# Seven block products in place of eight for part of a down projection, with one weight sum by an accumulating DMA

## The chip, the cores and the metric

The kernel runs on one core of a Trainium2 chip. The metric is the device time of one execution in microseconds; shown is the median of three runs. All values are 32-bit floats. The work is one layer of a streaming encoder for 256 tokens (two token tiles of 128) of width 2048.

## The reference

The layer is a set of token mixers with an output projection, then a feed-forward half with width 5632. The change touches the last product of the feed-forward half and what leads to it and from it:

```python
def rms_norm(x, g):
    return x * lax.rsqrt(jnp.mean(x * x, axis=-1, keepdims=True) + EPS) * g
...
h = h + rms_norm(mixed @ w_out, g_post_mix)
u = rms_norm(h, g_pre_ffn)
f = silu(u @ w_gate) * (u @ w_up)              # [256, 5632]
h = h + rms_norm(f @ w_down, g_post_ffn)       # w_down [5632, 2048]
```

## The kernel before

A product of 32-bit precision is made of three products of float32r parts: each operand is cut into a high part (a cast) and a low part (the operand less the high part), and the matmuls are high with high, high with low, low with high (`product`, lines 206 to 211).

All weights pass as one stream of chunks. A chunk is 256 rows by 512 columns, held as `[128, 2, 512]`, 512 KB. `load` (line 154) puts it into one of four buffers `raw` by a DMA on SP's queue; `prep` (line 158) makes its parts, in the down projection with one cast on ScalarE (line 168, tile `hi`) and one subtraction on VectorE (line 169, tile `lo`), into one of `NPARTS = 5` pairs. Each chunk feeds 12 matmuls: two token tiles, two rows of 128, three part products. When a chunk's matmuls are issued, `release` tops up the stream: the next chunk is prepared as long as it is less than five chunks ahead of the last released one, and loads run up to four chunks ahead of preparation. ScalarE, VectorE and TensorE take their instructions in the order in which the program issues them; the order on SP's and POOL's queues is set by a scheduler when the program is built.

Other work (evacuations, transposes, norms) is cut into steps by generators, which the class `Side` issues between chunks. In the feed-forward half, `up_job` (from line 1097) multiplies gate and up, transposes the result on TensorE into two PSUM banks and cuts it into the parts `fh[i]`, `fl[i]`, for each of the 11 row blocks `i` of 512 rows. `xt` holds the residual `h` in SBUF from the middle of the kernel to the end.

The down projection goes over four column blocks `b` of 512. For each, 22 chunks are multiplied into a pair of accumulators, one per token tile. `y_job` then squares the sums on ScalarE (line 1138) and multiplies them by the gain on VectorE (line 1141). In the last column block the last four chunks are taken for token tile 0 first and then for tile 1, so that the norm and the last step (`final`, line 1154) of tile 0 run beside the matmuls of tile 1.

## Time and profile before

| what | us |
|---|---|
| median of three runs | 1085.11 (1084.42 to 1085.63) |
| span of the profiled execution | 1084.9 |
| TensorE busy (matmuls) | 1071.0 |
| VectorE busy | 685.4 |
| ScalarE busy | 606.4 |
| 16 DMA engines, share of the span of the load queue | 57.2% |

The profile is of one execution. No time of its own is listed for it beside its span; the span lies among the three times, 0.2 us under their median. In the lines, PE is TensorE, PEld its weight load, DVE VectorE, ACT ScalarE, POOL GpSimd, and SP the engine that issues the loads (SPq is its queue). L168 is line 168 of the kernel. The page is read from the busy shares to the chain that ended last, and a stretch by its windows, its waits ("A waited for B: us in total, times, longest") and its timeline (start, duration, engine, line, operation, and the idle time ahead of it with what ended it).

### The profile page before, as it was taken

How to read it: one execution, taken by the hardware profiler on the slowest of the kernel's cores; microseconds unless marked ns; L12 is line 12 of the kernel's file. 1: busy time of each engine (PE TensorE's matmuls, PEld its weight loads, DVE VectorE, ACT ScalarE, POOL GpSimd, SP SyncE). 2: the span in 40 equal slices, each digit the busy share in tenths (PEclk: the TensorE clock that was granted, in tenths of full speed). 3: DMA queues.
4: the chain of work that ended last, by engine and by line, in shares of the span. 5: the costliest groups of instructions: out<-in, count | busy, mean ns of one | idle time of the engine just before them, and what ended most of it. 6: DMA issues, size and time to landing. Idle time of an engine off the chain costs nothing.

```text
span 1084.9 us, 13175 instructions
## 1 busy us (share of the span) xinstructions
PE 1071.0 (99%) x4826; PEld 887.6 (82%) x4826; DVE 685.4 (63%) x988; ACT 606.4 (56%) x867; POOL 8.8 (1%) x19
## 2 busy tenths in 40 slices
PE   8999999999999999999999999999999999999996
PEld 6888888888888888888888888888888888888885
DVE  6576998976687765665556656565565444444544
ACT  6768757678854855545455454555554434343432
POOL 0000001010000000000000000000000000000000
PEclk9999999999999999999999999999999999999998
DMA  8854554546572465555555555555556555565552
GB/s 313 293 188 157 186 175 155 194 166 214 194 236 94 155 227 183 192 194 184 185 194 192 192 183 190 194 189 193 183 192 218 194 195 193 194 193 194 194 192 78
DMA packets 58097, 207.03 MB, mean 191 GB/s; under 512 B 6448, under 2 KB 6832, under 8 KB 57776
## 3 DMA queue, kind: packets, MB, share of 16 engines
q1 hardware_dynamic: 58032, 206.18, 57.2%
q8 instruction: 38, 0.62, 0.2%
q14 instruction: 27, 0.22, 0.1%
HBM read 204.06 MB, written 2.10 MB: 190 GB/s over the span
## 4 chain that ended last, share of the span: by engine, by line
PE 98%; DMA 1%; DVE 0%; ACT 0%; SPq 0%; issue 0%; ACTq 0%
PE acc L209 32%; PE acc L210 32%; PE acc L211 32%; PE bank L1106 1%; PE bank L352 1%; DMA w<-xT 1%; PE bank L975 0%; PE bank L662 0%; PE bank L713 0%; DVE xt L1154 0%; PE bank L714 0%; PE bank L663 0%; PE bank L515 0%; PE bank L516 0%; PE bank L433 0%; PE bank L691 0%
## 5 line engine op out<-in xcount | busy, mean ns | idle before, releaser
L209 PE MATMUL acc<-hi,w 128*128 128x512 f32 x1360 | 533.4, 392 | 3.3 <-ACT hi L770 1.8
L210 PE MATMUL acc<-lo,w 128*128 128x512 f32 x1360 | 530.5, 390 | 0.3 <-DVE lo L771 0.3
L211 PE MATMUL acc<-hi,w 128*128 128x512 f32 x1360 | 530.6, 390 | 0.0
L169 DVE TENSOR_TENSOR lo<-raw,hi 128x1024 fp32r<-128x1024 f32 x198 | 241.6, 1223 | 186.9 <-ACT hi L168 186.3
L165 DVE SCALAR_TENSOR_TENSOR lo<-raw,par,hi 128x512 fp32r<-128x512 f32 x344 | 242.7, 748 | 184.7 <-ACT hi L164 184.7
L164 ACT ACTIVATE hi<-raw,par 128x512 fp32r<-128x512 f32 x344 | 229.5, 717 | 208.0 <-PE acc L211 208.0
L168 ACT CAST hi<-raw 128x1024 fp32r<-128x1024 f32 x198 | 207.0, 1050 | 211.5 <-PE acc L211 192.9
L209 PEld LDWEIGHTS acc<-hi,w 128*128 128x128 f32 x1360 | 256.0, 188 | 56.5 <-ACT hi L770 4.3
L211 PEld LDWEIGHTS acc<-hi,w 128*128 128x128 f32 x1360 | 255.8, 188 | 53.8 <-DVE w L982 0.5
L210 PEld LDWEIGHTS acc<-lo,w 128*128 128x128 f32 x1360 | 256.0, 188 | 53.3 <-DVE lo L771 1.2
L594 DVE SCALAR_TENSOR_TENSOR w<-u,par,w 128x256 f32<-128x256 f32 x120 | 51.1, 482 | 0.0
L209 PE MATMUL acc<-hi,mh 128*128 128x512 f32 x128 | 50.4, 394 | 0.0
L211 PE MATMUL acc<-hi,ml 128*128 128x512 f32 x128 | 49.9, 390 | 0.0
L210 PE MATMUL acc<-lo,mh 128*128 128x512 f32 x128 | 49.8, 389 | 0.0
L211 PEld LDWEIGHTS acc<-hi,ml 128*128 128x128 f32 x128 | 24.0, 188 | 5.1
L210 PEld LDWEIGHTS acc<-lo,mh 128*128 128x128 f32 x128 | 24.1, 188 | 4.8
L209 PEld LDWEIGHTS acc<-hi,mh 128*128 128x128 f32 x128 | 24.0, 188 | 4.8
L1095 DVE SCALAR_TENSOR_TENSOR s<-acc,rffn,s 128x512 f32<-128x512 f32 x22 | 15.4, 742 | 0.0
L1100 DVE SCALAR_TENSOR_TENSOR s<-acc,rffn,s 128x512 f32<-128x512 f32 x22 | 15.4, 742 | 0.0
L347 ACT ACTIVATE w<-acc,rpre 128x512 f32<-128x512 f32 x22 | 13.8, 684 | 2.2 <-DVE rpre L307 2.2
L1113 DVE TENSOR_TENSOR w<-bank,w 128x512 fp32r<-128x512 f32 x22 | 14.1, 682 | 0.0
L1092 ACT ACTIVATE s<-acc,rffn 128x512 f32<-128x512 f32 x22 | 13.7, 675 | 0.0
(204 smaller groups left out, 425.4 us busy)
## 6 DMA issues: line engine op xcount, KB each, us to landing
raw<-w_up SPq DMA_DIRECT2D x88, 512.0 KB, 3.3
raw<-w_down SPq DMA_DIRECT2D x88, 512.0 KB, 3.3
raw<-w_gate SPq DMA_DIRECT2D x84, 512.0 KB, 3.3
raw<-w_in SPq DMA_DIRECT2D x78, 512.0 KB, 3.4
raw<-w_out SPq DMA_DIRECT2D x32, 512.0 KB, 3.4
xt<-x_tok SPq DMA_DIRECT2D x2, 1024.0 KB, 7.9
w<-w_gate SPq DMA_DIRECT2D x4, 512.0 KB, 5.5
out<-xt SPq DMA_DIRECT2D x8, 256.0 KB, 2.1
```

What stands on the lines that cost most here:

```text
L164: A.activation(hi[:, kk, :], raw[:, kk, :], AF.Copy, scale=g)
L165: V.scalar_tensor_tensor(out=lo[:, kk, :], in0=raw[:, kk, :], scalar=g, in1=hi[:, kk, :].bitcast(F32), op0=ALU.mult, op1=ALU.subtract)
L168: A.copy(out=hi, in_=raw)
L169: V.tensor_tensor(out=lo, in0=raw, in1=hi.bitcast(F32), op=ALU.subtract)
L209: T.matmul(acc, xh(k)[:, ts], hi[:, kk, :], start=first, stop=False)
L210: T.matmul(acc, xh(k)[:, ts], lo[:, kk, :], start=False, stop=False)
L211: T.matmul(acc, xl(k)[:, ts], hi[:, kk, :], start=False, stop=last)
L347: A.activation(dst[:, t, :], acc[t], func, scale=rpre[:, t:t + 1])
L594: V.scalar_tensor_tensor(out=cy[:, n, :], in0=u[:, n, j:j + S], scalar=pv("dw_conv_w", j * 4 + n), in1=cy[:, n, :], op0=ALU.mult, op1=ALU.add)
L1095: V.scalar_tensor_tensor(out=ss[t], in0=acc[t], scalar=rffn[:, t:t + 1], in1=ss[t], op0=ALU.mult, op1=ALU.mult)
L1100: V.scalar_tensor_tensor(out=ss[t], in0=acc[t], scalar=rffn[:, t:t + 1], in1=ss[t], op0=ALU.mult, op1=ALU.mult)
L1113: V.tensor_tensor(out=fl[i][:, :, ts], in0=tp, in1=fh[i][:, :, ts].bitcast(F32), op=ALU.subtract)
```

## The change

The down projection takes its column blocks in two pairs. With the two token tiles and the two halves of a row block of 512, four row blocks (`SFORM`: 1, 3, 5 and 7 of 0 to 10) become products of 2 x 2 blocks, and these are computed as seven block products, named Q3, P7, P1, P6, P2, Q5 and R4, in place of eight. A block product is one token tile by 256 rows by 512 columns: 6 matmuls. Its operand from the activations is a block or a sum of blocks that `up_job` makes beside the usual parts (tiles `sh`, `sl` and a changed quarter of `fh`, `fl`). Its operand from the weights is a block or a sum of blocks, in four buffers x, y, z, u: Q3 takes w22 (y), P7 w12 + w22 (x), P1 w11 (z), P6 x + z (into x), P2 w21 (u), Q5 x - y (into y), R4 x + u (into x). The sum w12 + w22 is made by an accumulating DMA from POOL's queue on top of a plain load by SP; the other three by VectorE (`add`, issued between the cast and the low part of the item ahead). Each of the seven has its own cast and low part. `frees` gives a buffer back when the last low part that reads it is issued; the four places go round.

The seven products of the four row blocks are mingled with the plain chunks of the other seven row blocks: 6 plain chunks stand ahead and 4 behind in the first pair, 3 and 8 in the second. In the middle of each pair a block runs like this (s is a plain chunk): Q5 R4 s Q3 s P7 P1 s P6 s P2 Q5, then s R4 Q3 s P7 s P1 P6 s P2 s Q5.

P2, Q3 and R4 go straight into accumulators of plain products; P1, P6, P7 and Q5 have PSUM banks of their own, joined at the end of a pair by `sums_job` and `join_y`, ahead of square and gain. To make room, the residual is written to DRAM (`hsave`) after the middle norm, two of the operand sums lie in its place (`aside`), and `bring_back` reads it back during the last chunks.

```diff
+class Prod:
+    def __init__(self, group, name, ap, dst, add, frees, more=None):
+        self.group, self.name, self.ap, self.dst, self.add, self.frees = group, name, ap, dst, add, frees
+        self.more = more
+        self.has_load = ap is not None
+        self.added = add is None
+def seven(w11, w12, w21, w22, **at):
+    g = {"bufs": {}, **at}
+    return [
+        Prod(g, "Q3", w22, "y", None, ""),
+        Prod(g, "P7", w12, "x", None, "", w22),
+        Prod(g, "P1", w11, "z", None, ""),
+        Prod(g, "P6", None, "x", ("x", "x", "z", ALU.add), "z"),
+        Prod(g, "P2", w21, "u", None, ""),
+        Prod(g, "Q5", None, "y", ("y", "x", "y", ALU.subtract), "y"),
+        Prod(g, "R4", None, "x", ("x", "x", "u", ALU.add), "xu"),
+    ]
+def mingled(many, few, head, tail):
+    mid = few[head:len(few) - tail]
+    out, n = list(few[:head]), 0
+    for i, item in enumerate(many):
+        out.append(item)
+        while n * len(many) < (i + 1) * len(mid):
+            out.append(mid[n])
+            n += 1
+    return out + list(few[len(few) - tail:])
...
-    stream += [w_down[b, c] for b in range(4) for c in range(NFK // 2)]
+    stream = [Std(ap) for ap in stream]
     gate0 = (len(mixers) + 4) * 8
     down0 = gate0 + NFB * 16
+    plain = [n for n in range(NFK // 2) if n // 2 not in SFORM]
+    downs = []
+    for b, head, tail in ((0, 6, 4), (2, 3, 8)):
+        prods = [p for i in SFORM for p in seven(*(w_down[b + c, 2 * i + k] for k, c in ((0, 0), (0, 1), (1, 0), (1, 1))), i=i)]
+        downs.append(mingled(prods, [Std(w_down[b + c, n], b + c, n) for c in range(2) for n in plain], head, tail))
+    stream += downs[0] + downs[1]
...
     def load(i, raw=None):
+        item = stream[i]
+        if isinstance(item, Prod):
+            if item.has_load:
+                buf = item.group["bufs"][item.dst] = sraws.lend(NT, CB)
+                nc.sync.dma_start(out=buf, in_=item.ap)
+                if item.more is not None:
+                    G.dma_start(out=buf.rearrange("p a b -> p (a b)"), in_=item.more.rearrange("p a b -> p (a b)"), accum_op=ALU.add)
+            return
         raws[i] = wp.tile([P, 2, CB], F32, tag="raw", name="raw", bufs=NRAW) if raw is None else raw
-        nc.sync.dma_start(out=raws[i], in_=stream[i])
+        nc.sync.dma_start(out=raws[i], in_=item.ap)
+    def add(i):
+        item = stream[i] if i < len(stream) else None
+        if isinstance(item, Prod) and not item.added and i < at["load"]:
+            dst, a, b, op = item.add
+            bufs = item.group["bufs"]
+            V.tensor_tensor(out=bufs[dst], in0=bufs[a], in1=bufs[b], op=op)
+            item.added = True
...
             A.copy(out=hi, in_=raw)
+            add(i + 1)
             V.tensor_tensor(out=lo, in0=raw, in1=hi.bitcast(F32), op=ALU.subtract)
         parts[i] = (hi, lo)
+        if isinstance(item, Prod):
+            for n in item.frees:
+                sraws.back(item.group["bufs"].pop(n))
...
         if at["load"] < min(len(stream), at["prep"] + NRAW):
+            item = stream[at["load"]]
+            if isinstance(item, Prod) and item.has_load and not sraws.free:
+                return False
             load(at["load"])
             at["load"] += 1
+            return True
+        return False
...
+            if at["load"] <= i and not load_next():
+                return False
             prep(i)
         at["prep"] += 1
         load_next()
+        if i >= down0:
+            while load_next():
+                pass
         return True
...
+    for t in range(NT):
+        nc.sync.dma_start(out=hsave[t * P:(t + 1) * P, :], in_=xt[:, t, :])
...
+    sh, sl = {}, {}
+    sraws.free.extend(place(ffp, f"sr{n}") for n in range(2))
+    extra = [place(ffp, f"sf{n}", 768)(6, P, F32R) for n in range(4)]
+    aside = res.tile([P, 4, 6, P], F32R, tag="xt", name="aside")
+    for n, i in enumerate(SFORM):
+        sh[i], sl[i] = (extra[2 * n], extra[2 * n + 1]) if n < 2 else (aside[:, 2 * n - 4], aside[:, 2 * n - 3])
...
+        turned = [b.rearrange("p (c t) -> p c t", c=4) for b in tps]
+        if i in SFORM:
+            a11, a12, a21, a22 = (turned[t][:, k:k + 2, :] for t in range(NT) for k in (0, 2))
+            s1, s2, s3, s4 = (sums[:, n] for n in range(4))
+            yield 1.2, 0.96, 1
+            V.tensor_copy(out=s3, in_=a21)
+            V.tensor_tensor(out=s1, in0=s3, in1=a22, op=ALU.subtract)
+            V.tensor_tensor(out=s2, in0=s1, in1=a11, op=ALU.subtract)
+            V.tensor_tensor(out=s4, in0=s2, in1=a12, op=ALU.add)
+            V.tensor_tensor(out=s3, in0=a11, in1=s3, op=ALU.subtract)
+            split(fh[i][:, :, :P], fl[i][:, :, :P], turned[0])
+            yield 0.8, 0.6, 1
+            split(fh[i][:, 2:4, P:], fl[i][:, 2:4, P:], a22)
+            split(fh[i][:, 0:2, P:], fl[i][:, 0:2, P:], s1)
+            banks.back(*tps)
+            yield 1.0, 0.9, 0
+            split(sh[i], sl[i], sums.rearrange("p n k t -> p (n k) t")[:, 2:8, :])
+            return
...
-    def square_y(t, b, acc):
+    def square_y(t, b):
         junk = small.tile([P, CB], F32, tag="junk", name="junk", bufs=1)
-        A.activation(junk, acc, AF.Square, accum_out=ss2[:, t, b:b + 1])
-    def gain_y(t, b, acc):
-        V.tensor_tensor(out=y2[t][b], in0=acc, in1=gp2[b], op=ALU.mult)
-    def y_job(b, acc):
-        yield 1.2, 0.6, 1
-        for t in range(NT):
...
+    def y_job(b, banks_of):
+        while ("sums", b // 2 * 2) not in st:
+            yield WAIT
+        yield 1.4, 0, 1
+        for t in range(NT):
+            join_y(t, b, banks_of[t])
+        yield 1.2, 1.2, 1
+        for t in range(NT):
+            square_y(t, b)
+            gain_y(t, b)
         if b == 2:
             yield 0.6, 0, 1
             for t in range(NT):
                 partial(ss2, t)
 
+    def sums_job(b, ps):
+        (c11, c12), (c21, c22) = (y2[t][b:b + 2] for t in range(NT))
+        yield 0, 0.6, 0
+        A.copy(out=c11, in_=ps["P1"])
+        yield 0.7, 0, 0
+        V.tensor_tensor(out=c12, in0=ps["P6"], in1=c11, op=ALU.add)
+        yield 0.7, 0, 0
+        V.tensor_tensor(out=c21, in0=ps["P7"], in1=c12, op=ALU.add)
+        yield 0.7, 0, 0
+        V.tensor_tensor(out=c22, in0=ps["Q5"], in1=c21, op=ALU.subtract)
+        yield 0.7, 0, 0
+        V.tensor_tensor(out=c12, in0=ps["Q5"], in1=c12, op=ALU.subtract)
...
     def final(t, b):
-        V.scalar_tensor_tensor(out=xt[:, t, cols(b)], in0=y2[t][b], scalar=rout[:, t:t + 1], in1=xt[:, t, cols(b)],
-                               op0=ALU.mult, op1=ALU.add)
-        nc.sync.dma_start(out=out[t * P:(t + 1) * P, cols(b)], in_=xt[:, t, cols(b)])
...
+        h = kept["xt"][:, t, cols(b)]
+        V.scalar_tensor_tensor(out=h, in0=y2[t][b], scalar=rout[:, t:t + 1], in1=h, op0=ALU.mult, op1=ALU.add)
+        nc.sync.dma_start(out=out[t * P:(t + 1) * P, cols(b)], in_=h)
+    def form(name, i):
+        def of_f(k, t):
+            return [tuple(f[i][:, k + kk, t * P:(t + 1) * P] for f in (fh, fl)) for kk in range(2)]
+        def of_s(n):
+            return [tuple(f[i][:, 2 * n + kk, :] for f in (sh, sl)) for kk in range(2)]
+        return {"P1": lambda: of_f(0, 0), "P2": lambda: of_f(2, 0), "R4": lambda: of_f(2, 1), "Q5": lambda: of_f(0, 1),
+                "P6": lambda: of_s(0), "P7": lambda: of_s(1), "Q3": lambda: of_s(2)}[name]()
...
+    def uses(b, item):
+        if isinstance(item, Std):
+            return [((t, item.b - b), std_form(item.n, t)) for t in range(NT)]
+        to = {"P2": (0, 0), "Q3": (0, 1), "R4": (1, 0)}.get(item.name, item.name)
+        return [(to, form(item.name, item.group["i"]))]
+    for f in ("hl2", "hl3"):
+        sraws.free.append(place(hlp, f))
+    NLAST = 4
+    kept = {}
+    def bring_back():
+        kept["xt"] = res.tile([P, NT, D], F32, tag="xt", name="xt")
+        for t in range(NT):
+            nc.sync.dma_start(out=kept["xt"][:, t, :], in_=hsave[t * P:(t + 1) * P, :])
...
+        last_prod = max(n for n, x in enumerate(order) if isinstance(x[0], Prod))
+        bank, own = {}, []
...
+        for n, (item, to, tiles) in enumerate(order):
+            if b and n == len(order) - NT * len(tail):
+                side.need(*yjobs)
+                warm_root()
+            if isinstance(item, Prod):
+                side.need(*([last_up] if b == 0 else yjobs[:2]))
+            if item not in ws:
+                ws[item] = take()
+            w, out_bank = ws[item], bank_of(to)
+            for kk in range(2):
+                (xhi, xlo), (hi, lo) = tiles[kk], w
+                T.matmul(out_bank, xhi, hi[:, kk, :], start=n == first[to] and kk == 0, stop=False)
+                T.matmul(out_bank, xhi, lo[:, kk, :], start=False, stop=False)
+                T.matmul(out_bank, xlo, hi[:, kk, :], start=False, stop=n == end[to] and kk == 1)
+            if n == last_prod:
+                sj = side.add(0, sums_job(b, bank))
+                if b:
+                    bring_back()
+            for c in range(2):
+                if n == max(end[t, c] for t in range(NT)) and b + c < 3:
+                    yjobs.append(side.add(0, y_job(b + c, [bank[t, c] for t in range(NT)])))
+            if n + 1 == len(order) or order[n + 1][0] is not item and item not in tail:
+                side.slot()
+                release()
+        if b == 0:
+            side.need(sj)
...
+        join_y(t, 3, bank[t, 1])
+        square_y(t, 3)
+        gain_y(t, 3)
         close_rms(rout, ss2, t)
         for b in range(4):
-            if b == 3:
-                gain_y(t, 3, acc[t])
             final(t, b)
```

In the down projection before, VectorE makes one low part for each chunk, with nothing else between:

```order
L169 TENSOR_TENSOR lo_8374<-raw_8305,hi_8373 128x1024
L169 TENSOR_TENSOR lo_8392<-raw_8323,hi_8391 128x1024
L169 TENSOR_TENSOR lo_8410<-raw_8341,hi_8409 128x1024
L169 TENSOR_TENSOR lo_8428<-raw_8359,hi_8427 128x1024
L169 TENSOR_TENSOR lo_8446<-raw_8377,hi_8445 128x1024
```

In the changed kernel, from Q5 of row block 1 to P6 of row block 3 in the first pair, this stands on VectorE. `w_6977` is y of block 1 (read by Q5), `w_7013` its x (R4), and `w_7208`, `w_7235`, `w_7254` are y, x and z of block 3 (read by Q3, P7, P1); L229 is a sum, L249 a low part.

```order
L249 TENSOR_TENSOR lo_7218<-w_6977,hi_7217 128x1024
L249 TENSOR_TENSOR lo_7232<-w_7013,hi_7231 128x1024
L249 TENSOR_TENSOR lo_7251<-raw_7189,hi_7250 128x1024
L249 TENSOR_TENSOR lo_7263<-w_7208,hi_7262 128x1024
L249 TENSOR_TENSOR lo_7281<-raw_7222,hi_7280 128x1024
L249 TENSOR_TENSOR lo_7292<-w_7235,hi_7291 128x1024
L249 TENSOR_TENSOR lo_7304<-w_7254,hi_7303 128x1024
L229 TENSOR_TENSOR w_7235<-w_7235,w_7254 128x1024
L249 TENSOR_TENSOR lo_7322<-raw_7266,hi_7321 128x1024
L249 TENSOR_TENSOR lo_7333<-w_7235,hi_7332 128x1024
```

Between the low parts of plain chunks now stand those of the products, and a sum ahead of P6's; the low part of `w_7235`, and its cast on ScalarE, stand behind the accumulating DMA.

SP's queue in the down projection before holds loads of plain chunks alone:

```order
L156 DMA raw_7763<-w_down 128x1024
L156 DMA raw_7781<-w_down 128x1024
L156 DMA raw_7799<-w_down 128x1024
L156 DMA raw_7825<-w_down 128x1024
L156 DMA raw_7843<-w_down 128x1024
```

After, in the same place as above, loads of u, x and z of the next row block stand among them (L216); that of `w_7235` waits for the low part of `w_6977`, and the one of `w_7254` for the next low part:

```order
L221 DMA raw_7295<-w_down 128x1024
L216 DMA w_7307<-w_down 128x1024
L216 DMA w_7235<-w_down 128x1024
L216 DMA w_7254<-w_down 128x1024
L221 DMA raw_7336<-w_down 128x1024
L221 DMA raw_7377<-w_down 128x1024
```

POOL's queue has the accumulating DMAs, the first for row block 1 and the second on top of the load of `w_7235`, for which it waits:

```order
L218 DMA w_7013<-w_down 128x1024
L218 DMA w_7235<-w_down 128x1024
L218 DMA w_7396<-w_down 128x1024
```

So one load a chunk has become, for a row block, four loads by SP and one accumulating DMA behind one of them.

## Rows read from the trace of the kernel before

**Rows 1.** The page: busy time of each engine, and the chain by engine.
```profile
PE 1071.0 (99%) x4826; PEld 887.6 (82%) x4826; DVE 685.4 (63%) x988; ACT 606.4 (56%) x867; POOL 8.8 (1%) x19
...
PE 98%; DMA 1%; DVE 0%; ACT 0%; SPq 0%; issue 0%; ACTq 0%
```
**Rows 2.** Windows of the feed-forward products and the down projection.
```profile
core 0: us, PE busy (x) PEld busy (x) DVE busy (x) ACT busy (x) POOL busy (x), PEclk, DMA share, GB/s
540.00:830.00 290.00, 290.00 (x1305) 240.55 (x1304) 172.26 (x246) 153.03 (x234) 0.00 (x0) 1.00 0.58 191
840.00:1060.00 220.00, 220.00 (x976) 182.26 (x975) 104.08 (x93) 89.42 (x95) 0.00 (x0) 1.00 0.58 192
```
**Rows 3.** Waits in the down projection: in total us, times, longest.
```profile
ACT hi L168 <- PE acc L211: 132.5, 82, 1.7
DVE lo L169 <- ACT hi L168: 118.4, 83, 1.5
...
SPq L156 <- DVE lo L169: 181.0, 78, 3.2
```
**Rows 4.** Timeline of ScalarE and VectorE, down projection: start, duration, engine, operation.
```profile
1040.72 1.05 ACT L168 CAST hi<-raw 128x1024 fp32r<-128x1024 f32 x1 [1.67 <-PE acc L211]
1043.44 1.05 ACT L168 CAST hi<-raw 128x1024 fp32r<-128x1024 f32 x1 [1.67 <-PE acc L211]
1046.16 1.05 ACT L168 CAST hi<-raw 128x1024 fp32r<-128x1024 f32 x1 [1.67 <-PE acc L211]
...
1041.81 1.23 DVE L169 TENSOR_TENSOR lo<-raw,hi 128x1024 fp32r<-128x1024 f32 x1 [1.50 <-ACT hi L168]
```
**Rows 5.** Groups on VectorE by shape, whole span: busy us, mean ns.
```profile
L169 DVE TENSOR_TENSOR lo<-raw,hi 128x1024 fp32r<-128x1024 f32 x198 | 241.6, 1223 | 186.9 <-ACT hi L168 186.3
...
L1113 DVE TENSOR_TENSOR w<-bank,w 128x512 fp32r<-128x512 f32 x22 | 14.1, 682 | 0.0
...
L684 DVE TENSOR_TENSOR w<-w 128x768 fp32r<-128x768 f32 x4 | 4.0, 1001 | 0.0
...
L699 DVE TENSOR_TENSOR w<-w,bank 128x256 f32<-128x256 f32 x4 | 1.6, 409 | 0.0
...
L539 DVE TENSOR_TENSOR w<-w 128x1024 f32<-128x1024 f32 x1 | 1.2, 1226 | 0.0
...
L537 DVE TENSOR_SCALAR w<-w 128x1024 f32<-128x1024 f32 x1 | 0.7, 689 | 0.0
```
**Rows 6.** The page: DMA issues with count, KB each, us to landing.
```profile
raw<-w_down SPq DMA_DIRECT2D x88, 512.0 KB, 3.3
...
xt<-x_tok SPq DMA_DIRECT2D x2, 1024.0 KB, 7.9
w<-w_gate SPq DMA_DIRECT2D x4, 512.0 KB, 5.5
out<-xt SPq DMA_DIRECT2D x8, 256.0 KB, 2.1
```
**Rows 7.** Timeline of ScalarE and VectorE at the end of the span.
```profile
1070.64 0.60 ACT L1138 ACTIVATE junk<-acc 128x512 f32<-128x512 f32 x1 [5.59 <-PE acc L211]
...
1076.14 0.60 ACT L1138 ACTIVATE junk<-acc 128x512 f32<-128x512 f32 x1 [4.33 <-PE acc L211]
...
1071.36 0.21 DVE L921 TENSOR_SCALAR cr<-ss,spre 128x1 f32<-128x1 f32 x1 [6.57 <-ACT junk L1138]
...
1072.68 2.08 DVE L1154 SCALAR_TENSOR_TENSOR xt<-w,rout,xt 128x512 f32<-128x512 f32 x3
1074.68 0.68 DVE L1141 TENSOR_TENSOR w<-acc,w 128x512 f32<-128x512 f32 x1
...
1080.89 0.75 DVE L1154 SCALAR_TENSOR_TENSOR xt<-w,rout,xt 128x512 f32<-128x512 f32 x1
```
**Rows 8.** Tile raw, down projection: the loads of weights, us from issue to landing.
```profile
DMA to landing us min/median/max: 3.1/3.3/4.5
```

More of the change, by code (lines that the diff above doesn't have):

```diff
@@ L1086, in block_kernel @@
               [place(xs, f"x1{2 * n + i}")(4, S, F32R) for i in range(2)] for n in range(2))
-    ss = [ffp.tile([P, CB], F32, name=f"s{t}") for t in range(NT)]
+    both = place(ffp, "s")(NT, CB)
+    ss = [both[:, t, :] for t in range(NT)]
+    sums = both.rearrange("p t c -> p (t c)").rearrange("p (n k t) -> p n k t", n=4, t=P)
+    sh, sl = {}, {}
[4 more added lines that the diff above has]
+        sh[i], sl[i] = (extra[2 * n], extra[2 * n + 1]) if n < 2 else (aside[:, 2 * n - 4], aside[:, 2 * n - 3])
     def silu_job(acc):
@@ L1095, in silu_job, with split @@
             V.scalar_tensor_tensor(out=ss[t], in0=acc[t], scalar=rffn[:, t:t + 1], in1=ss[t], op0=ALU.mult, op1=ALU.mult)
+    def split(hi, lo, src):
+        A.copy(out=hi, in_=src)
+        V.tensor_tensor(out=lo, in0=src, in1=hi.bitcast(F32), op=ALU.subtract)
     def up_job(i, acc):
@@ L1110, in up_job @@
             ts = slice(t * P, (t + 1) * P)
-            tp = tps[t].rearrange("p (c t) -> p c t", c=4)
-            A.copy(out=fh[i][:, :, ts], in_=tp)
-            V.tensor_tensor(out=fl[i][:, :, ts], in0=tp, in1=fh[i][:, :, ts].bitcast(F32), op=ALU.subtract)
+            split(fh[i][:, :, ts], fl[i][:, :, ts], turned[t])
         banks.back(*tps)
@@ L1128, in block_kernel @@
     gp2 = [None] * 4
+    for b in range(0, 4, 2):
+        both = place(hlp, f"hl{b // 2}")(NT, CB)
+        nc.sync.dma_start(out=both.rearrange("p t c -> p (t c)"), in_=g_post2[:, b * CB:(b + 2) * CB].broadcast_to([P, 2 * CB]))
+        gp2[b], gp2[b + 1] = both[:, 0, :], both[:, 1, :]
     for b in range(4):
-        gp2[b] = place(hlp, f"hl{b}")(1, CB)[:, 0, :]
-        nc.sync.dma_start(out=gp2[b], in_=g_post2[:, cols(b)].broadcast_to([P, CB]))
         both = place(xs, f"x0{b}")(NT, CB)
@@ L1165, in block_kernel @@
-    block(acc, ff, kf[:-8], last=False)
-    side.need(yj)
-    warm_root()
-    r = rows(kf[-8:], [take() for _ in range(4)])
+    def sums_job(b, ps):
[11 more added lines that the diff above has]
+        if b == 0:
+            banks.back(*(ps[n] for n in ("P1", "P6", "P7", "Q5")))
+        st["sums", b] = True
@@ new lines, in std_form @@
+    def std_form(n, t):
+        return [tuple(f[n // 2][:, 2 * (n % 2) + kk, t * P:(t + 1) * P] for f in (fh, fl)) for kk in range(2)]
+    def uses(b, item):
[6 more added lines that the diff above has]
+    NLAST = 4
@@ new lines, in block_kernel, with bank_of @@
+    kept = {}
[3 more added lines that the diff above has]
+            nc.sync.dma_start(out=kept["xt"][:, t, :], in_=hsave[t * P:(t + 1) * P, :])
+    yjobs = []
+    for b, items in zip((0, 2), downs):
+        tail = items[len(items) - NLAST:] if b else []
+        order = [(item, *use) for item in items[:len(items) - len(tail)] for use in uses(b, item)]
+        order += [(item, *uses(b, item)[t]) for t in range(NT) for item in tail]
+        first, end = {}, {}
+        for n, (_, to, _) in enumerate(order):
+            first.setdefault(to, n)
+            end[to] = n
+        last_prod = max(n for n, x in enumerate(order) if isinstance(x[0], Prod))
+        bank, own = {}, []
+        def bank_of(to):
+            if to not in bank:
+                if isinstance(to, tuple) == (b == 0):
+                    if b == 0:
+                        bank[0, to[1]], bank[1, to[1]] = acc_pair()
+                    else:
+                        if not own:
+                            own.extend(acc_pair() + acc_pair())
+                        bank[to] = own.pop(0)
+                else:
+                    bank[to] = banks.lend()
+            return bank[to]
+        ws = {}
+        for n, (item, to, tiles) in enumerate(order):
+            if b and n == len(order) - NT * len(tail):
+                side.need(*yjobs)
+                warm_root()
+            if isinstance(item, Prod):
+                side.need(*([last_up] if b == 0 else yjobs[:2]))
[17 more added lines that the diff above has]
+                release()
+        if b == 0:
+            side.need(sj)
```

40 lines of the change are left out of this document (22 added, 18 removed).

## The prediction, made before the change was run

> **What bounds the kernel now.** I read the page's busy shares and chain first, then the stretch that is changed by windows, waits, groups and timeline. TensorE is busy 99% of the span and holds 98% of the chain that ended last [rows 1]. In the down projection it never pauses: 220.0 of 220 us busy, granted clock 1.00 (the 2.4 GHz level), with VectorE at 104 and ScalarE at 89 us [rows 2]. Who waits there says the same: ScalarE's cast of a chunk waited 82 times for a matmul (132.5 us) and never for a DMA; VectorE waits for the cast, and the load queue for VectorE (181.0 us) [rows 3]. So weights come early, and only what shortens TensorE's own list, or makes it wait, moves the end. One chunk is 12 matmuls and its casts start 2.72 us apart, at 1040.72, 1043.44 and 1046.16 [rows 4]: 0.2267 us a matmul.
>
> **What is removed.** Of the 11 row blocks of 512, four go through seven block products in place of eight, in each of two pairs of column blocks. A block product is 6 matmuls, so 4 x 2 x 6 = 48 matmuls fall away (in the built programs 4769 against 4721). 48 x 0.2267 = **10.9 us**, all on the path.
>
> **What is added beside other work.** (a) In the feed-forward half, a seven-product block's up step issues on VectorE one copy and four additions of 256 elements (0.41 each by the nearest row), and its low parts as pieces of 512, 256, 256 and 768 elements (0.68, 0.41, 0.41, 1.0) in place of two of 0.68: 2.05 + 2.5 - 1.36 = 3.2 us more, four times. VectorE is 59% busy there [rows 2, 5], five chunks of parts lie ready, 13.6 us of matmuls: nothing. If that cover were gone it would cost 13 us. (b) Storing the residual to DRAM adds two 1 MB DMAs on SP's queue, at 7.9 us each by the nearest row [rows 6]. The loads behind them run nine chunks ahead, 24 us: nothing. (c) Reading it back: SP waits for the last matmul that reads the area lent to the sums (138 matmuls from the end, 31 us), with five of the last loads queued behind. The first of these is needed 78 matmuls, 17.7 us, after the release. The first read and that load are 7.9 + 3.3, and cast and low part 2.3 more: 13.5, so hidden. The fifth, behind both reads, comes by 2 x 7.9 + 5 x 1.6 + 2.3 = 26.1 at worst and is needed at 24.5 us: I take nothing, and 1.6 us as the bound. (d) The end: a join (0.68) now stands ahead of each square, and the gain (0.68) leaves the chain, since it runs beside the square. Before, the last matmul ends at 1076.14 and the last VectorE step at 1081.64, 5.5 us. After, token half 0 is ready 5.5 us before that end, and join 0.70, square 0.72, closing steps 1.32 and four last steps 2.75 make 5.5, so VectorE is just free; the second half takes the same 5.5 [rows 7]. Net 0.
>
> **What may stand on the path: the sums of weights.** Of the sixteen sums in a pair of columns twelve are VectorE's, three a block (1.225 each by a 128x1024 addition [rows 5]), and four the accumulating DMA's, one a block. VectorE's capacity suffices: in the mixed stretch 46 low parts and 12 sums are 71 us beside 28 x 1.36 + 18 x 2.72 = 87 us of matmuls. What may not suffice is a loop. The buffer for w12 + w22 of the next block (product P7) comes free when the low part of Q5 of this block is done. Only then SP loads w12, POOL waits for that load and adds w22, and ScalarE's cast of P7 waits for POOL's DMA. Behind that cast every later cast stands in order, on VectorE the low parts, and then TensorE. I call L the time from that low part to the landed sum.
>
> *Around the loop.* From the landed sum to the next Q5's low part the order gives one cast (1.05) and 9 or 11 VectorE instructions of 1.225, with 0.04 between: 12.4 or 14.8 us [rows 4, 5]. TensorE has, from P7 to the next P7, 7 products and 4 or 5 plain chunks: 20.4 or 23.1 us. So the two laps of a pair leave L room for 20.4 - 12.4 = 8.0 and 23.1 - 14.8 = 8.3 us in the first pair, and in the second, by its own order, 23.1 - 14.8 = 8.3 and 20.4 - 12.3 = 8.1.
>
> *The entry.* The first block's sum is loaded far ahead. Preparation runs at most five items ahead of TensorE, so its Q5 is prepared when TensorE starts the item four before. By the order a plain chunk's low part ends 0.9 us after that moment, R4's sum at 2.1 and Q5's low part at 3.4 us. The four items take 8.16 us, and from Q5 to P7 of the second block are 9.52 us in the first pair (Q5, R4, a chunk, Q3, a chunk) and 6.8 in the second (one chunk fewer): P7 starts 17.7 or 15.0 us after that moment and needs cast and low part, 2.15 us, before. Room for L: 12.1 and 9.4 us.
>
> *The stall* over the three exposed sums of a pair is the room overdrawn: 3L - (12.1 + 8.0 + 8.3) = 3L - 28.4 and 3L - (9.4 + 8.3 + 8.1) = 3L - 25.8, where positive. Nothing up to L = 8.6; from 9.5 on 6L - 54.2, so it eats the 10.9 at L = 10.85. One microsecond of L is six of the kernel.
>
> *L itself.* No accumulating DMA and no DMA issued from POOL stands in the trace of before, so it is bounded. A load lands 3.3 us after its issue [rows 6]. That of w12 is the third of five loads that VectorE's steps release 1.2 us apart, where each keeps all DMA engines for 1.6 us (512 KB at 192 GB/s and a share of 0.58 [rows 2]): 0.7 us more, 4.0. An accumulate is at best a load, 3.3, which gives L = 7.4 with two hops between engines (0.04 each [rows 4]); at worst 7.9, the 1 MB row, behind a load of 5.5, a crowded one: L = 13.5. It reads twice its bytes (the weights and the buffer), so I price it as 1 MB in a calm queue: 256 KB took 2.1 us and 512 KB 3.3, 1.2 for each further 256 KB, so 3.3 + 2.4 = 5.7 [rows 6]. L = 4.0 + 5.7 + 0.1 = **9.8 us**, between the ends and nearer to the calm one, since the loads here landed calmly at 3.1 to 4.5 [rows 8]. Stall 1.0 + 3.6 = **4.6 us**.
>
> **The sum.** 1084.9 (span) - 10.9 + 4.6 = 1078.6; the median of the runs lies 0.2 above that span: **1078.8 us**.
>
> A rule speaks against the change. VectorE's 128x1024 TENSOR_SCALAR took 0.689 us where TENSOR_TENSOR of that shape took 1.225 [rows 5]; the fast form stands nowhere between the sums of the down projection, only the slow one. The Trainium skill (SBUF — State Buffer, Who interferes with whom) says that such fast two-port forms lock GpSimd out, so that it can't write descriptors, and infers that tensor_tensor does not. If it did, L would grow by up to one 1.225 us step, the time by 7.3 to about 1086: that would be the even case below, whose chance holds it. No run here shows it yet.
>
> **Rivals.** *Hidden (L up to 8.6).* For it: ScalarE has not once waited for a weight DMA here [rows 3], and the DMA engines are 58% busy. Against: the sum now starts only after a free buffer and a landed load. No stall: 1074.2. The Trainium skill (DMA: Bandwidth & Descriptors, Anatomy of one DMA) gives 2.0 us plus bytes at 436 GB/s for a DMA from GpSimd; as an estimate, with the bytes doubled, that is 4.4 us, L = 8.4 and this rival.
>
> *Even (L 10.5 to 11.2).* The stall, 8.7 to 13.1, gives the gain back: about 1085.
>
> *Slower (L above 11.2).* The accumulate in the loop, at the rate of the crowded rows, takes TensorE's place as the bound. It decides at the third sum of each pair, where the overdraft is largest. At L = 12.0 the stall is 17.8 and the time 1092.0; at 13.5 it is 26.8, 1101. For it: two DMAs in series and the buffer's reuse in one lap, loads bunched around them. Against: the calm landings [rows 8].
>
> *It does not do what it says:* the matmuls that are left would have to run slower than 0.2267. They keep their shape, and the clock is 1.00 throughout; I give this nothing of its own, though long stalls might lower the clock.
>
> **How the numbers follow.** Forecast (L 8.6 to 10.5) 0.38; hidden 0.22; even 0.15; slower 0.25. Within 0.2% (2.2 us, about what a measurement of this kernel can tell from no change) is even: faster 0.60, same 0.15, slower 0.25. The range goes from 1073.5, the hidden case with half a microsecond to spare, to 1092, L = 12.0; it leaves out about 0.15 of slower and little below.
>
> **What would show it.** In the profile after: 48 fewer matmuls at the same spacing; TensorE waits in two clusters, at the second to fourth P7 of each pair, longer in the second, released by the cast or low part of a summed buffer, whose cast waits for POOL's DMA; L read from the low part of Q5 to that landing. If the accumulate lands within 5 us of its issue, hidden; over 7, slower. I am wrong if TensorE waits elsewhere: at the pairs' border for banks, behind the residual's DMAs, or all along for VectorE; or if L is as said and TensorE does not wait.

## The result, and the profile after

The change made the kernel slower. The median is 1101.8 us (four runs, 1097.9 to 1105.4) against 1084.8 (four runs beside it); the ratio is 1.0153, 95% interval [1.0137, 1.0169]. Two of the four runs took 1097.9 and 1098.9 us and two 1104.7 and 1105.4; the profile is of the one with 1098.9, and its span is 1097.2.

The 48 matmuls are gone, but TensorE waits and the chain that ended last now holds DMAs and vector work, as the page of the changed kernel shows (busy us, then the chain by engine; compare [rows 1]):

```profile
PE 1071.4 (98%) x4778; PEld 883.6 (81%) x4778; DVE 758.5 (69%) x1080; ACT 631.6 (58%) x901; POOL 16.0 (1%) x27
...
PE 85%; DMA 6%; DVE 4%; ACT 2%; issue 2%; SPq 0%; DVEq 0%; ACTq 0%; POOLq 0%
```

The two stretches of [rows 2], then four pieces of the second, in the changed kernel (the columns are those of [rows 2]):

```profile
540.00:830.00 290.00, 290.00 (x1305) 240.63 (x1304) 179.17 (x264) 156.09 (x240) 0.00 (x0) 1.00 0.60 193
840.00:1060.00 220.00, 208.43 (x874) 168.67 (x873) 152.44 (x137) 104.40 (x111) 6.17 (x7) 0.95 0.61 190
...
900.00:920.00 20.00, 17.99 (x66) 14.31 (x67) 16.34 (x14) 12.17 (x12) 0.00 (x0) 0.83 0.57 188
980.00:1000.00 20.00, 16.54 (x65) 12.91 (x64) 10.00 (x10) 7.38 (x8) 0.89 (x1) 0.91 0.58 170
...
1020.00:1040.00 20.00, 19.73 (x80) 16.16 (x81) 15.24 (x14) 8.87 (x9) 0.88 (x1) 0.91 0.65 204
1040.00:1060.00 20.00, 17.27 (x63) 13.37 (x62) 14.81 (x13) 10.65 (x11) 0.00 (x0) 0.83 0.46 147
```

The feed-forward half is as full as before. In the down projection TensorE is idle for 220 - 208.4 = 11.6 us, and the granted clock falls in the four pieces shown: (0.17 + 0.09 + 0.09 + 0.17) x 20 = 10.4 us of lost clock. VectorE is at 152 of 220 us, so it isn't the bound by its mean.

The waits of that stretch (total us, times, longest) have a line that [rows 3] did not have, ScalarE's cast waiting for a DMA into a buffer `w`, which is one of the four places of the sums. The last two lines are TensorE's own waits for a cast, four in all:

```profile
DVE lo L249 <- ACT hi L247: 68.1, 27, 9.8
...
ACT hi L247 <- DMA w<-w_down: 37.1, 4, 10.0
ACT hi L247 <- DVE w L229: 30.0, 20, 1.9
ACT hi L247 <- PE acc L1378: 29.8, 19, 5.8
...
PE acc L1376 <- ACT hi L247: 6.4, 3, 2.7
...
PE bank L1376 <- ACT hi L247: 2.3, 1, 2.3
```

One such wait at TensorE, the timeline of PE at P7 of block 5 in the second pair (start, duration):

```profile
1019.01 0.49 PE L1376 MATMUL acc<-hi,aside 128*128 128x512 f32 x1 [1.43 <-ACT hi L247]
1020.27 0.50 PE L1377 MATMUL acc<-lo,aside 128*128 128x512 f32 x1 [0.77 <-DVE lo L249]
...
1020.99 0.63 PE L1376 MATMUL acc<-hi,aside 128*128 128x512 f32 x1
...
1023.55 0.63 PE L1376 MATMUL acc<-hi,w 128*128 128x512 f32 x1
...
1024.47 0.39 PE L1376 MATMUL bank<-hi,w 128*128 128x512 f32 x1
```

TensorE waits 1.43 us for the cast and 0.77 for the low part. The matmuls behind the wait last 0.63 us in place of 0.39 and start 0.43 us apart, the 1.2 GHz level; from 1024.24 on they are back at 0.39 and 0.23. Four waits of this kind stand in the stage: at P7 of block 5 in the first pair (2.34 us for the cast, 0.47 for the low part, from 901.55 on) and at P7 of blocks 3, 5 and 7 in the second. At blocks 3 and 7 of the first pair TensorE started P7 without a gap and waited only 0.3 and 0.4 us longer than usual for the low part of the plain chunk behind P7 and P1 (at 881.45 and 931.62). The expectation of run 1 counts six waits; it is six late casts, but four waits.

**The loop, read in the trace.** The lap behind the wait above, then the lap ahead of P7 of block 7 in the first pair, on all engines but TensorE. The first row is two low parts, of which the first (to 1.22 us after the start) frees the buffer; the load of w12 is the second of the three in the next row. The last cast below is put down to TensorE, as is the one of block 3 in that pair, but both started 0.1 to 0.2 us after the accumulation had landed (5.4 and 5.5 us from POOL's start):

```profile
1003.00 2.50 DVE L249 TENSOR_TENSOR lo<-w,hi 128x1024 fp32r<-128x1024 f32 x2
1003.11 2.74 SPq L216 DMA_DIRECT2D w<-w_down  x3
...
1010.53 0.87 POOL L218 DMA_DIRECT2D w<-w_down  x1 [26.21 <-DMA w<-w_down]
1017.91 1.04 ACT L247 CAST hi<-w 128x1024 fp32r<-128x1024 f32 x1 [8.71 <-DMA w<-w_down]
```
```profile
913.03 2.51 DVE L249 TENSOR_TENSOR lo<-w,hi 128x1024 fp32r<-128x1024 f32 x2
913.14 2.75 SPq L216 DMA_DIRECT2D w<-w_down  x3
...
920.19 0.89 POOL L218 DMA_DIRECT2D w<-w_down  x1 [27.93 <-DMA w<-w_down]
925.85 2.00 ACT L247 CAST hi<-w 128x1024 fp32r<-128x1024 f32 x2 [5.82 <-PE acc L1378]
```

The prediction's L is the time from the freed buffer to the landed sum; it is read here to the cast that starts 0.1 to 0.2 us later. All six (load: freed to POOL's start; accumulation: POOL's start to the cast; beside it: what SP's queue moved in that time):

| pair, block of P7 | load, us | accumulation, us | L, us | beside it, MB |
|---|---|---|---|---|
| 1, 3 | 6.2 | 5.5 | 11.7 | 0.64 |
| 1, 5 | 4.0 | 9.1 | 13.1 | 1.87 |
| 1, 7 | 5.9 | 5.7 | 11.6 | 0.73 |
| 2, 3 | 6.3 | 7.0 | 13.2 | 0.23 |
| 2, 5 | 6.3 | 7.4 | 13.7 | 0.79 |
| 2, 7 | 5.2 | 8.7 | 13.9 | 1.65 |
| sum | 33.9 | 43.3 | 77.2 | |

The prediction's formula, stall = sum of the six L - 54.2, gives 77.2 - 54.2 = **23.0 us**. Between the last matmul of the changed kernel, at 1086.18, and that of the same kernel without the loop (first experiment), at 1063.10, lie **23.1**. By pairs the formula gives 8.0 and 15.0; at equal matmuls the changed kernel was 6.9 us behind the other after the first pair, and so 16.2 fell in the second. How much of that agreement is luck is said further down.

### The profile page after: what moved, and what is told of

The parts are those of the page before. It is cut to its first block, busy times and chain, and to the rows that moved or that the text cites. A ratio compares the mean times of both kernels' runs of the same rounds, so it can differ in the third digit from the quotient of the medians.

```text
span 1097.2 us, 13279 instructions
## 1 busy us (share of the span) xinstructions
PE 1071.4 (98%) x4778; PEld 883.6 (81%) x4778; DVE 758.5 (69%) x1080; ACT 631.6 (58%) x901; POOL 16.0 (1%) x27
## 4 chain that ended last, share of the span: by engine, by line
PE 85%; DMA 6%; DVE 4%; ACT 2%; issue 2%; SPq 0%; DVEq 0%; ACTq 0%; POOLq 0%
PE acc L300 24%; PE acc L301 24%; PE acc L302 24%; DMA w<-w_down 5%; DVE lo L249 2%; PE acc L1377 2%; PE acc L1378 2%; PE acc L1376 2%; ACT hi L247 2%; PE bank L1376 2%; PE bank L1377 2%; PE bank L1378 2%; DVE w L229 1%; PE bank L1214 1%; DMA raw<-w_in 1%
## 5 line engine op out<-in xcount | busy, mean ns | idle before, releaser
L300 PE MATMUL acc<-hi,w 128*128 128x512 f32 x1008 | 396.1, 393 | 1.3 <-DVE w L431 1.2
L301 PE MATMUL acc<-lo,w 128*128 128x512 f32 x1008 | 393.5, 390 | 0.7 <-DVE lo L249 0.5
L302 PE MATMUL acc<-hi,w 128*128 128x512 f32 x1008 | 393.2, 390 | 0.0
L249 DVE TENSOR_TENSOR lo<-raw,hi 128x1024 fp32r<-128x1024 f32 x166 | 202.0, 1224 | 84.0 <-ACT hi L247 83.1
L247 ACT CAST hi<-raw 128x1024 fp32r<-128x1024 f32 x166 | 172.3, 1048 | 109.0 <-PE acc L302 51.2
L301 PEld LDWEIGHTS acc<-lo,w 128*128 128x128 f32 x1008 | 189.7, 188 | 40.8 <-DVE lo L249 1.2
L300 PEld LDWEIGHTS acc<-hi,w 128*128 128x128 f32 x1008 | 189.6, 188 | 40.7 <-ACT hi L863 2.3
L302 PEld LDWEIGHTS acc<-hi,w 128*128 128x128 f32 x1008 | 189.6, 188 | 40.0 <-DVE w L1075 0.5
L247 ACT CAST hi<-w 128x1024 fp32r<-128x1024 f32 x56 | 58.0, 1050 | 88.4 <-DMA w<-w_down 37.1
L249 DVE TENSOR_TENSOR lo<-w,hi 128x1024 fp32r<-128x1024 f32 x56 | 67.8, 1223 | 52.8 <-ACT hi L247 51.0
L1376 PE MATMUL acc<-hi,w 128*128 128x512 f32 x156 | 62.8, 402 | 2.7 <-ACT hi L247 2.7
L1377 PE MATMUL acc<-lo,w 128*128 128x512 f32 x156 | 62.5, 401 | 1.2 <-DVE lo L249 1.0
L1378 PE MATMUL acc<-hi,w 128*128 128x512 f32 x156 | 62.2, 399 | 0.0
L1376 PE MATMUL bank<-hi,w 128*128 128x512 f32 x156 | 61.4, 394 | 0.0
L1377 PE MATMUL bank<-lo,w 128*128 128x512 f32 x156 | 61.3, 393 | 0.0
L1378 PE MATMUL bank<-hi,w 128*128 128x512 f32 x156 | 60.9, 391 | 0.0
## 6 DMA issues: line engine op xcount, KB each, us to landing
xt<-x_tok SPq DMA_DIRECT2D x2, 1024.0 KB, 8.1
```

The costliest lines, as they stand in the source:

```text
L247: A.copy(out=hi, in_=raw)
L249: V.tensor_tensor(out=lo, in0=raw, in1=hi.bitcast(F32), op=ALU.subtract)
L300: T.matmul(acc, xh(k)[:, ts], hi[:, kk, :], start=first, stop=False)
L301: T.matmul(acc, xh(k)[:, ts], lo[:, kk, :], start=False, stop=False)
L302: T.matmul(acc, xl(k)[:, ts], hi[:, kk, :], start=False, stop=last)
L1376: T.matmul(out_bank, xhi, hi[:, kk, :], start=n == first[to] and kk == 0, stop=False)
```

## The experiments

Theory A: the loop of the buffers, with L as read, makes the whole loss. Theory B: the DMA engines or VectorE are too full, and the accumulation is only one load among others. Theory C: the residual's way through DRAM or the tail. Theory D: the half clock is a loss of its own beside the waits. The runs of before that stood beside them had medians of 1085.3.

**1. The sum by VectorE.**

```diff
-        Prod(g, "P7", w12, "x", None, "", w22),
+        Prod(g, "P7", w12, "x", ("x", "x", "y", ALU.add), ""),
```

> The sum of weights for the product P7 is made by VectorE out of two plain loads, as the other three sums are; the accumulating DMA is gone, VectorE has 8 more additions of about 1.22 us, and nothing else is changed. Theory A, the loop of the buffers: what made TensorE wait is the way from a buffer's release by Q5's low part through the load and the accumulation to P7's cast, 11.7 to 13.1 us where it was read in the changed kernel. With the two loads it is 4 to 6 us plus an addition of 1.2, within the room, so the six waits of 1.2 to 3.2 us ahead of P7 go, the half clock behind them goes too, and the time falls from 1101.8 to 1074 to 1079 us. Theory B, the engines are too full: the DMA engines or VectorE (which gets 10 us more work in a stretch where it was already the fullest engine after TensorE) set the pace; then the time stays at 1095 to 1105 us, with waits of TensorE ahead of all products and not of P7 alone.

Measured: 1075.24 us, ratio to before 0.991 [0.9895, 0.9925]. Its window of the down projection, and the one wait there for a load into a place of the sums:

```profile
840.00:1060.00 220.00, 220.00 (x977) 182.24 (x976) 178.04 (x166) 118.68 (x126) 0.00 (x0) 1.00 0.56 189
```
```profile
DVE w L229 <- DMA w<-w_down: 6.2, 4, 2.5
```

TensorE is full and the clock 1.00, though VectorE now has 178 of 220 us, 26 more than in the changed kernel over a stretch that holds more of the work. A full VectorE was not the cause, and B loses that half. VectorE still waits for a load of the loop, but by 2.5 us at most, and TensorE never sees it.

**2. No accumulation at all.**

```diff
-        Prod(g, "P7", w12, "x", None, "", w22),
+        Prod(g, "P7", w12, "x", None, ""),
```

> The accumulating DMA is left out and nothing takes its place: P7 is multiplied with one weight block where the sum of two belongs, so that part of the computation (the second block in this one sum) is missing; all matmuls, casts and other loads are as they were. Theory A (the loop of the buffers): the waits ahead of P7 go as in the run with VectorE's sum and the time is 1073 to 1078 us, at most 2 us under that run. Theory C, the reading back of the residual, the longer tail or the first sums of the activations make the loss: then taking the accumulation away gives back less than 10 us and the time stays over 1090 us.

Measured: 1075.15 us (two runs), ratio 0.9908 [0.9888, 0.9928], the same as with VectorE's sum. Everything of the change but the accumulation is in this kernel: the residual's store and return, the longer up steps, the tail, four buffers, 32 loads in bunches. Together they leave 10.2 us of gain (1085.34 - 1075.15), so theory C falls, and VectorE's 8 additions of run 1 have no price.

**3. The accumulation twice.**

```diff
+                    G.dma_start(out=buf.rearrange("p a b -> p (a b)"), in_=item.more.rearrange("p a b -> p (a b)"), accum_op=ALU.add)
```

> The accumulating DMA into P7's buffer is issued twice, one after the other, so that the sum holds the second block twice; the rest is unchanged. Theory A: every lap of the loop grows by one more accumulation, 5.4 to 9.2 us as read in the changed kernel; on six laps that is 32 to 55 us of waiting, and the time goes to 1132 to 1160 us (more if TensorE is granted the half clock for longer). Theory B (the DMA engines' throughput): 8 more accumulations at about 2.9 us of all 16 engines are 23 us more of DMA work in a stretch that had room for it, and the time rises by under 15 us.

Measured: 1134.67 us (two runs), ratio 1.0456 [1.043, 1.0482], 32.9 over the changed kernel's median. One lap in its timeline, with both accumulations of P7 of block 5 in the first pair; then the queues while the second one ran:

```profile
896.39 0.88 POOL L218 DMA_DIRECT2D w<-w_down  x1 [20.31 <-DVE lo L250]
...
906.71 0.89 POOL L219 DMA_DIRECT2D w<-w_down  x1 [9.45 <-DMA w<-w_down]
912.13 1.04 ACT L248 CAST hi<-w 128x1024 fp32r<-128x1024 f32 x1 [14.76 <-DMA w<-w_down]
```
```profile
DMA  0000000000099909194949999295999949010000
...
q0 software_dynamic: 144, 0.52, 58.8%
issues: line engine op xcount, KB each, median us to landing
w<-w_down POOLq DMA_DIRECT2D x1, 512.0 KB, 5.3
```

The second accumulation took 5.4 to 5.7 us in all six exposed laps, 33.4 together, and the first ones were longer than in the changed kernel, 49.1 together against 43.3; 33.4 + 5.8 is 39.2. Counted from the 301st matmul, near the start of the program, the last matmul came 39.3 us later than in the trace of the changed kernel (1124.68 - 73.07 against 1086.18 - 73.86): a microsecond in the loop is a microsecond of the kernel in each lap. (That the medians lie 32.9 apart, close to 33.4, is chance: the changed kernel's lies between its two kinds of run.) Theory B, which counts engine time, 0.588 x 5.4 = 3.2 us for each, allowed 15.

The run also bears on what makes an accumulation long. Five of the second ones found the load queue empty (in the list above no other queue stands), the sixth 0.08 MB on it. The first ones took 5.8, 10.3, 8.7, 7.3, 7.5 and 9.4 us with 0.79, 1.75, 0.95, 0.18, 0.79 and 1.49 MB of loads beside them. The longest stand beside the most loads, but 7.3 us beside 0.18 MB, like 7.0 beside 0.23 at the same place in the changed kernel, is not explained by that.

**4. Five places in place of four.** The accumulation stays; a tile that is unused in this stage is lent as the fifth place, and the stream may run eight items ahead.

```diff
-        if at["load"] < min(len(stream), at["prep"] + NRAW):
+        if at["load"] < min(len(stream), at["prep"] + (NRAW if at["prep"] < down0 else 2 * NRAW)):
...
+            if isinstance(item, Std) and len(raws) >= NRAW:
+                return False
...
+    sraws.free.append(place(ffp, "s"))
```

> The accumulating DMA stays, with its length and its bytes; the four places for the sums of weights become five, and the stream is allowed to run 8 items ahead instead of 4 in the down projection, so that P7's load starts when P6's addition has freed a buffer and no longer when Q5's low part has. Theory A: the room of a lap grows by some 7 us, to about 15, which is over the 11.7 to 13.1 us that load and accumulation took; the waits ahead of P7 go and the time is 1074 to 1080 us. Theory B (the accumulating DMA crowds the engines or is too dear in itself): it moves the same bytes, so the waits stay and the time is 1095 us or more.

Measured: 1075.73 us, ratio 0.9911 [0.9894, 0.9927]. The accumulations of this kernel on the page (KB, us to landing), its window of the down projection, and its casts' wait:

```profile
w<-w_down POOLq DMA_DIRECT2D x8, 512.0 KB, 7.1
```
```profile
840.00:1060.00 220.00, 220.00 (x976) 182.30 (x976) 170.05 (x158) 119.06 (x125) 6.18 (x7) 1.00 0.66 207
```
```profile
ACT hi L247 <- DMA w<-w_down: 1.4, 1, 1.4
```

The accumulations are nearly as long as before (7.1 against 7.9 us) and the engines move more in the stretch (share 0.66 against 0.61), yet TensorE never waits. The same DMA with the same bytes costs nothing once its buffer comes free earlier. That is theory A against B, in the cleanest form.

**5. The control: eight items ahead, four places.**

```diff
-        if at["load"] < min(len(stream), at["prep"] + NRAW):
+        if at["load"] < min(len(stream), at["prep"] + (NRAW if at["prep"] < down0 else 2 * NRAW)):
...
+            if isinstance(item, Std) and len(raws) >= NRAW:
+                return False
```

> The control for the run with five places: the stream may run 8 items ahead in the down projection, but the four places stay four. Theory A (places, not the stream's limit, hold P7's load back): as the changed kernel, 1097 to 1106 us, with the waits ahead of P7. If the limit of 4 items held the load back, the waits shrink and the time falls below 1090 us.

Measured: 1098.33 us (two runs), ratio 1.0119 [1.0098, 1.0139]; the casts' wait is there:

```profile
ACT hi L247 <- DMA w<-w_down: 49.5, 6, 10.3
```

So it was the place, not the permission to load further ahead.

**6. TensorE kept busy through the waits.**

```diff
+    zero_r = const.tile([P, P], F32R, name="zero_r")
+    A.activation(zero_r, ones, AF.Copy, scale=0.0)
...
+            if isinstance(item, Prod) and item.name == "P7" and item.group["i"] > 1:
+                for _ in range(12):
+                    T.matmul(out_bank.rearrange("p (a t) -> p a t", a=2), zero_r, fh[0][:, 0:2, :], start=False, stop=False)
```

> The changed kernel with 12 matmuls of a block of zeros added into P7's own bank ahead of P7 in blocks 3, 5 and 7 of each pair of column blocks (6 x 12, 2.7 us each time at 0.2267 us), so that TensorE works on through most of the wait for P7's cast and the granted clock should stay at 1.00 behind it. Theory A, the loop alone: the way from release to cast and on to the next release sets the lap, the half clock of the changed kernel lay inside it, and only the last lap's, with nothing behind it, comes back: a gain of 0 to 4 us, 1098 to 1103 us. Theory D, the half clock is a loss of its own beside the waits: about 9 us come back, less up to 3 us by which the added matmuls outlast the waits: 1092 to 1096 us.

Measured: 1099.04 us, ratio 1.0126 [1.011, 1.0141]. Two of its windows (the same columns as above), and its timeline of PE at P7 of block 7, second pair:

```profile
900.00:920.00 20.00, 20.00 (x90) 16.48 (x89) 16.35 (x14) 11.20 (x12) 0.00 (x0) 1.00 0.56 180
...
1040.00:1060.00 20.00, 18.36 (x78) 14.27 (x77) 12.79 (x12) 9.02 (x10) 0.00 (x0) 1.00 0.49 154
```
```profile
1043.61 2.97 PE L1378 MATMUL acc<-w,zero_r 128*128 128x512 f32 x12
1047.05 0.49 PE L1381 MATMUL acc<-hi,aside 128*128 128x512 f32 x1 [0.48 <-ACT hi L247]
1048.31 0.50 PE L1382 MATMUL acc<-lo,aside 128*128 128x512 f32 x1 [0.77 <-DVE lo L249]
```

The clock stays at 1.00 where it had been 0.83, and the time is that of the profiled run of the changed kernel, 1098.9, and of the control, 1098.3. Counted from the 301st matmul, the last one came 1.3 us sooner than in the changed kernel (1086.80 - 75.78 against 1086.18 - 73.86), within theory A's 0 to 4. The added matmuls are 72 x 0.2267 = 16.3 us against 11.6 of idle time, so they can hide 4.7 us of a gain; 1.3 and 4.7 are 6.0, short of D's 9 and of the 10.4 of lost clock. And at P7 of blocks 5 and 7 of the second pair TensorE, at full clock and behind the added matmuls, still waited 0.24 and 0.48 us for the cast. So theory D falls as a loss of its own size, and most of the lost clock lay inside the laps: had TensorE gone faster, it would have stood longer at the next P7. There the lap was set by load, accumulation and the VectorE steps to the next release, and idle time and half clock are mostly the two forms in which TensorE spent the difference.

**7. The tail.** VectorE's sum as in run 1, and the last gain into a place of its own.

```diff
-        gain_y(t, 3)
+        V.tensor_tensor(out=gp2[t], in0=y2[t][3], in1=gp2[3], op=ALU.mult)
+        y2[t][3] = gp2[t]
```

> VectorE makes P7's sum, and at the end of the program the gain of the last column block is written to a place of its own in place of over its input, so that it needn't wait for ScalarE's square, which reads the same input. In the run with VectorE's sum alone the gain waited 0.85 us for the square twice, and 7.3 us lay between the last matmul's start and VectorE's end, against 6.0 in the kernel before. If that wait made the longer tail, each tile's chain shortens by about 0.6 to 0.85 us, and the time is 1.2 to 1.7 us under that run's 1075.2, so 1073.5 to 1074 us. If the tail is longer for the residual that was read back, or for the joining addition alone, the time stays within 0.5 us of 1075.2.

Measured: 1073.78 us, ratio 0.989 [0.9874, 0.9907], 1.46 under run 1. The tail of token tile 1 in the changed kernel, then in this one (start, duration; the last row is the four last steps):

```profile
1087.29 0.68 DVE L1267 TENSOR_TENSOR w<-bank,w 128x512 f32<-128x512 f32 x1
1088.06 0.63 ACT L1264 ACTIVATE junk<-w 128x512 f32<-128x512 f32 x1 [4.30 <-DVE w L1267]
...
1088.82 0.69 DVE L1270 TENSOR_TENSOR w<-w 128x512 f32<-128x512 f32 x1 [0.85 <-ACT junk L1264]
1089.42 0.21 DVE L1014 TENSOR_SCALAR cr<-ss,spre 128x1 f32<-128x1 f32 x1
...
1090.74 2.74 DVE L1306 SCALAR_TENSOR_TENSOR xt<-w,rout,xt 128x512 f32<-128x512 f32 x4
```
```profile
1064.31 0.68 DVE L1267 TENSOR_TENSOR w<-bank,w 128x512 f32<-128x512 f32 x1
1065.03 0.69 DVE L1394 TENSOR_TENSOR w<-w 128x512 f32<-128x512 f32 x1
1065.09 0.63 ACT L1264 ACTIVATE junk<-w 128x512 f32<-128x512 f32 x1 [4.30 <-DVE w L1267]
...
1065.85 0.22 DVE L1014 TENSOR_SCALAR cr<-ss,spre 128x1 f32<-128x1 f32 x1
...
1067.17 2.74 DVE L1306 SCALAR_TENSOR_TENSOR xt<-w,rout,xt 128x512 f32<-128x512 f32 x4
```

In the changed kernel the gain writes over the tile that the square reads, so it waits 0.85 us for ScalarE and delays the closing steps. With its own place it runs beside the square. From the last matmul's start to VectorE's end: 1093.48 - 1086.18 = 7.3 us in the changed kernel, 1069.91 - 1063.81 = 6.1 here, 6.0 in the kernel before. This version beats both kernels.

## Why the prediction was wrong

Right were the bound, the removed term and the mechanism. TensorE's own list was the bound, and with the loop open the last matmul starts 12.6 us earlier than before (1063.10 against 1075.65). Of these, 10.9 are the 48 matmuls. The other 1.6 are not the change: they stand already at the 301st matmul (74.08 against 75.70), arise in the first 30 us of the program, and differ between executions (the 301st matmul started at 73.86 in the changed kernel and at 75.78 in run 6). Counted from there, run 1 is 10.9 us ahead of the kernel before, the changed kernel 12.4 behind it, and the stall is 23.3. The waits stand at P7s behind a cast that waits for POOL's DMA, longer in the second pair, as described, though in the first pair only the third P7 waited long. Run 3 confirmed the slope.

The formula of the stall, at the measured L, held to 0.3 us in the sum and to 1.2 us in each pair, but in part by luck, since two errors cancel. VectorE's steps in the laps start 1.14 us apart (901.53, 902.67 and 903.80), where 1.225 with 0.04 between was priced, so that the way from P7's cast to the next freed buffer took 11.7 and 13.8 us in the first pair and 13.8 and 11.7 in the second, in place of 12.4, 14.8, 14.8 and 12.3: 3.3 us of room that the formula lacks, and with it 19.7 us as an estimate. For the second pair's two laps this is exact: 13.7 + 13.8 - 23.1 = 4.4 and 13.9 + 11.7 - 20.4 = 5.2, as TensorE's lag grew from P7 to P7. What fills the sum up to 23.3 is mostly the half clock, which the prediction gave nothing of its own: behind the last P7 nothing follows that could wait, and there the matmuls up to 1051.1 start 0.43 us apart in place of 0.23, 2.6 us together.

Wrong was the size of **L: 9.8 us in the prediction, 11.6 to 13.9 in the trace, 12.9 in the mean**. Both terms were too small:

- *The load*: 4.0 predicted, 5.6 in the mean of the six (33.9 / 6). The page after shows the loads of the stage crowded (KB, us to landing; compare [rows 6]):

```profile
raw<-w_down SPq DMA_DIRECT2D x56, 512.0 KB, 4.3
...
w<-w_down SPq DMA_DIRECT2D x32, 512.0 KB, 5.2
w<-w_down POOLq DMA_DIRECT2D x8, 512.0 KB, 7.9
```

  In run 1, without the accumulation, the two loads take 3.5 and 4.8: most of what a `w` load takes over the calm 3.3 is there without any accumulation, and goes with the bunch in which VectorE releases it.
- *The accumulation*: 5.7 predicted, 7.2 in the mean. Priced as a calm 1 MB it is right for a calm queue: 5.4 to 5.7 with next to nothing beside it in run 3, and 5.5 and 5.7 in two laps here with 0.6 and 0.7 MB of loads beside it. In the other four it took 7.0 to 9.1, between 5.7 and the 7.9 of the 1 MB row, and over that; the two longest had 1.7 and 1.9 MB beside them.

The step that failed is the choice between the bounds: "nearer to the calm one, since the loads here landed calmly" [rows 8]. Those calm loads came singly, one in 2.7 us. The change itself bunches them, several within a few microseconds, and puts a DMA of twice the engine time among them, just in the loop where it counts. The crowded end, 13.5, resembled the new stage; four of the six L lie within 0.4 us of it. With the measured L the prediction's own sum is 1084.9 - 10.9 + 23.0 = 1097.0 of span, against 1097.2 measured; the rival *slower* had the mechanism, the place and nearly the price, and a chance of 0.25 was too small.

Smaller points. **Tail (d)**, net 0 predicted: +1.8 us of span behind the last matmul (1097.2 - 1086.18 = 11.0, before 1084.9 - 1075.65 = 9.25). The failed step is "it runs beside the square": the gain is written in place, and run 7 gave 1.46 of it back by the medians, 1.2 by the traces. The early start (1.8 at the 301st matmul) and the tail cancel, which, beside the two errors in the stall, is why the sum above comes so close: that is luck. **(a), (b), (c)** cost nothing, as predicted: VectorE's 179 us in 290 leave TensorE full, run 2 holds all three, and TensorE is busy 20.00 of 20 us from 1060 to 1080 in the changed kernel. **The clock**: "long stalls might lower the clock" was right as an event, but it was given no price; 2.6 us of it lay behind the last P7, and run 6, without it, ran 1.3 us sooner in all.

The rule that was weighed against the change: POOL's issue of an accumulation lasted 0.87 to 0.89 us in all seven accumulations from 840 us on. In five of them VectorE was in the middle of a TENSOR_TENSOR (at 920.19, for one, within the low part from 920.06 to 921.29), in the two at 983.43 and 1010.53 it was idle, and the issue took the same time; POOL's spans are rough in the profile. What the Trainium skill infers there (SBUF — State Buffer, Who interferes with whom), that tensor_tensor does not lock GpSimd out, agrees. The estimate of 4.4 us from the Trainium skill (DMA: Bandwidth & Descriptors, Anatomy of one DMA) for the accumulation was under every measured one: 5.4 to 5.7 with next to no loads beside it, 10.3 at most (run 3).

**Open.** What the 6 us between the two lower and the two higher runs of the changed kernel are isn't settled; their mean granted clocks lay close together (0.987 and 0.990 against 0.985), and run 6 and the control lay at 1098 to 1100. That loads beside it make an accumulation long rests on the comparison within run 3 and on what the queues moved; the loads were not moved away as an experiment of its own, and the 7.0 and 7.3 us beside about 0.2 MB have no cause here.

## What to carry to other kernels

When a reused buffer closes a loop (freed, load, second DMA, cast, work, freed), add up the lap and compare it with the lap of the bound engine: every microsecond over is paid in each lap, however idle the DMA engines are in the mean. Price each DMA in such a loop by rows of a crowded moment, because the release that starts it starts its neighbours too; then give the loop one more buffer, or take the second DMA out of it. And a wait of the bound engine in a loop is not repaired by speeding that engine up.
